# Issuing the product of queries and state straight behind the products of the inverse, in a gated-delta and attention trunk

## The chip, the cores and the metric

The kernel runs on one core of a Trainium2 chip, in one launch. The metric is the device time of an execution in microseconds. The time before is the median of three runs. The engines are named as in the profile: PE is TensorE (PEld its weight loads), DVE is VectorE, ACT is ScalarE, POOL is GpSimd, SP is the engine that issues the DMAs. Each engine takes its instructions in the order in which they stand in its queue, and holds at an instruction whose semaphore has not come yet.

## What is computed

One sequence of 1024 tokens with 1024 channels goes through two layers. The first is a gated DeltaNet layer (16 value heads of width 128, 8 key heads, each of which serves two value heads), the second a forgetting-attention layer; both have a gate path, an output projection and a conditioning by adaLN. The change concerns the scan of the first layer:

```python
def step(state, inp):
    q_n, k_n, u_n, w_n, a_n, gl_n = inp
    v_new = u_n - jnp.einsum('bhcd,bhde->bhce', w_n, state)
    o = (jnp.einsum('bhcd,bhde->bhce', q_n, state)
         + jnp.einsum('bhcs,bhse->bhce', a_n, v_new))
    state = state * gl_n[..., None, None] + jnp.einsum('bhcd,bhce->bhde', k_n, v_new)
    return state, o
```

Here `u` and `w` come out of the inverse of a unit triangular matrix, of which there is one for each head and chunk. All of it is float32.

## The kernel before

The tokens are taken in two halves of 512, and the value heads in pairs that share a key head (8 groups). So the first layer has 16 units of work, one for each half and group, and each unit has four chunks of 128 tokens. For a unit the kernel projects k, q, v and the gate (float32 split into two float32r parts, three products each, tile `mm`), convolves them, builds the triangular matrices, inverts them by blocks (partly by DVE and small DMAs, then by `invert_merge` on PE), and at last runs `chain`, which walks through the four chunks with the state of the group.

In `chain` a chunk uses one bank of PSUM called `ch`, of which there is only one buffer. Its left half (columns 0 to 255) first takes the product of keys and state (L1000). DVE reads that half and makes `xp` (L1004). Two products with the blocks of the inverse, `r`, fill the right half (L1011). ACT reads the right half and makes `vn` (L1018), DVE reads it and makes `ve` (L1022). Then the product of queries and state is written to the left half (L1027), and ACT scales it into `qe` (L1031). A second bank, `co`, takes the two products with `vn` (L1039) and the product of keys with `ve` (L1041), from which DVE makes the new state (L1048) and the output of the chunk, `og` (L1056). Accesses to one bank by different engines are kept one after another, also where they touch different columns of it; the semaphores for that follow from the order in which the accesses stand in the program.

PE's order is set by hand, by the planner `Flow`. Each piece of work is a generator that yields a planned distance in ns; `Flow` adds a planned cost for every product and resumes, by priority, whichever generator is due. The distances behind the steps of a chunk are `Y_C0` = 2700 (behind `xp`), `Y_C1` = 2200 (behind the product of queries and state), `Y_C3` = 1300 (behind the products with `vn`) and `Y_C2` = 1700 (behind the state). Between the steps the planner puts projection products and other units' work. PE thus goes through a fixed list. The orders of DVE, ACT, POOL and SP are not written by hand: a scheduler sets them from a simulated run of the whole program.

Of the kernel before, what the change touches and what calls it, by code (L numbers as in the profile page):

```python
# [28 lines left out]
def bc(ap, axis, n):  # L29
    a = ap.unsqueeze(axis)  # L30
    shape = list(a.shape)
    shape[axis] = n
    return a.broadcast_to(shape)
# [74 lines left out]
class Flow:  # L108
# [21 lines left out]
    def mm(self, out, lhsT, rhs, start=True, stop=True):  # L130
        self.t += self._cost(lhsT, rhs)
        self.nc.tensor.matmul(out, lhsT, rhs, start=start, stop=stop)  # L132
# [54 lines left out]
def tile_trunk(  # L187
# [27 lines left out]
    mm, tr_ = flow.mm, flow.tr  # L215
# [297 lines left out]
    with ExitStack() as sa:  # L513
# [3 lines left out]
        def at(shape, name, bufs=1, dt=F32):  # L517
            return pa.tile(shape, dt, name=name, tag=name, bufs=bufs)

        def pst(tag, bufs):  # L520
            return flow.bank(tag, bufs, lambda: psa.tile([P, 512], F32, name=tag, tag=tag, bufs=bufs))
# [351 lines left out]
        def chain_all():  # L873
            for i in range(2 * NG):
                yield from hold(lambda: done["merge"] > i and done["prep2"] > i and done["prep"] > i)
                yield from chain(ts[i])
# [110 lines left out]
        def chain(t):  # L987
            h, g, gt, kf, r = t["h"], t["g"], t["gt"], t["k"], t["r"]
            ktok, qf, am, uv, epo, ex = t["ktok"], t["q"], t["am"], t["uv"], t["epo"], gt["ex"]
            wn, wex, neg = t["wn"], t["wex"], gt["neg"]  # L990
            st = state[g]
            og = at([P, CPH, 2, P], "og", 2)
            so = at([P, CPH, 2], "so", 2)
            for c in range(CPH):
                first = h == 0 and c == 0
                p1 = yield from pst("ch", 1)
                if first:
                    xp = uv[:, c].rearrange("p j f -> p (j f)")
                else:
                    mm(p1[:, 0:256], kf[:, c], st)  # L1000
                    xt = at([P, 2 * P], "xp", 2)
                    for j in range(2):
                        sl = slice(j * P, (j + 1) * P)
                        nc.vector.scalar_tensor_tensor(  # L1004
                            xt[:, sl], p1[:, sl], neg[:, c, 2 * g + j : 2 * g + j + 1], uv[:, c, j],
                            op0=ALU.mult, op1=ALU.add,
                        )
                    xp = xt
                    yield Y_C0
                for j in range(2):  # L1010
                    mm(  # L1011
                        p1[:, 256 + j * P : 256 + (j + 1) * P], r[:, j * CPH + c],
                        xp[:, j * P : (j + 1) * P],
                    )
                vn = at([P, 2 * P], "vn", 2)
                ve = at([P, 2, P], "ve", 2)
                for j in range(2):
                    nc.scalar.activation(  # L1018
                        vn[:, j * P : (j + 1) * P], p1[:, 256 + j * P : 256 + (j + 1) * P], AF.Copy,
                        scale=wn[:, c, j : j + 1],  # L1020
                    )
                nc.vector.tensor_tensor(  # L1022
                    ve, p1[:, 256:512].rearrange("p (j f) -> p j f", f=P),
                    bc(wex[:, c], 2, P), op=ALU.mult,
                )
                if not first:
                    mm(p1[:, 0:256], qf[:, c], st)  # L1027
                    qe = at([P, 2 * P], "qe", 2)
                    for j in range(2):
                        sl = slice(j * P, (j + 1) * P)  # L1030
                        nc.scalar.activation(  # L1031
                            qe[:, sl], p1[:, sl], AF.Copy, scale=ex[:, 1, c, 2 * g + j : 2 * g + j + 1]
                        )
                flow.free(p1, R_C + 1000)
                yield Y_C1
                p2 = yield from pst("co", 1)
                for j in range(2):
                    sl = slice(j * P, (j + 1) * P)
                    mm(p2[:, sl], am[:, j, c], vn[:, sl])  # L1039
                yield Y_C3  # L1040
                mm(p2[:, 256:512], ktok[:, c], ve.rearrange("p j f -> p (j f)"))  # L1041
                for j in range(2):
                    sl = slice(j * P, (j + 1) * P)
                    s2 = p2[:, 256 + j * P : 256 + (j + 1) * P]
                    if first:
                        nc.vector.tensor_copy(st[:, sl], s2)
                    else:
                        nc.vector.scalar_tensor_tensor(  # L1048
                            st[:, sl], st[:, sl], ex[:, 2, c, 2 * g + j : 2 * g + j + 1], s2,
                            op0=ALU.mult, op1=ALU.add,  # L1050
                        )
                oc = og[:, c].rearrange("p j f -> p (j f)")
                if first:
                    nc.scalar.copy(oc, p2[:, 0:256])
                else:
                    nc.vector.tensor_tensor(oc, p2[:, 0:256], qe, op=ALU.add)  # L1056
                for j in range(2):
                    jk = at([P, P], "sqt", 1, BF16)
                    nc.scalar.activation(jk, og[:, c, j], AF.Square, accum_out=so[:, c, j : j + 1])
                flow.free(p2, R_C)  # L1060
                yield Y_C2
            done["core"] += 1
            t["out"] = og, so
# [833 lines left out]
```

## Time and profile before

| | |
|---|---|
| median of 3 runs | 2116.97 us (2114.73 to 2119.29) |
| profiled execution | 2123.97 us, of which the span is 2122.0 |
| PE busy | 1885.7 us, 89% of the span |
| PEld busy | 1571.7 us, 74% |
| DVE busy | 1343.5 us, 63% |
| ACT busy | 1035.7 us, 49% |
| mean granted clock of PE | 0.947 |
| products of `ch`, first to last start | 185.4 to 1221.2 us |

In the profile all products stand under line L132 and all transposes under L136, the lines of the planner's two helpers, so they are told apart by the tiles that they write and read: `ch<-state,q` is the product of queries and state, `ch<-state,k` that of keys and state, `ch<-xp,rmat` those with the inverse. A float32 product makes two records, a float32r product one. "Idle before" is the time for which an engine had nothing to do ahead of an instruction, and the name behind the arrow is what ended it.

### The profile page before, as it was taken

Reading aid. Unit: us, or ns where it says so; the run is one execution under the profiler, and the core shown is the slowest. Engines: PE = TensorE matmul, PEld = TensorE weight load, DVE = VectorE, ACT = ScalarE, POOL = GpSimd, SP = SyncE. Lnnn points to the kernel's source line nnn. Section 1 sums busy time; section 2 is a strip of 40 time slices with the busy share of each in tenths; the row PEclk is TensorE's granted clock in tenths of the full one; section 3 lists DMA queues with packets and bytes.
Section 4 is the critical chain, followed back from the end, with each engine's and each line's share of the span. In section 5 each row is a group of like instructions: output and inputs, shape, how many; then the busy total and the mean of one; then the engine's idle time right before and its main releaser. Section 6 shows DMA issues by size and latency. Waiting matters only on the chain. (4 is left out here: it accounts for less than half of the span.)

```text
span 2122.0 us, 35794 instructions
## 1 busy us (share of the span) xinstructions
PE 1885.7 (89%) x12892; PEld 1571.7 (74%) x12892; DVE 1343.5 (63%) x3321; ACT 1035.7 (49%) x2672; POOL 367.1 (17%) x402
## 2 busy tenths in 40 slices
PE   4999798887888888888888888999999999999898
PEld 4777677666766676667766666878898888889676
DVE  6676877676667556756564556746666566566764
ACT  4455566454544344535444335426556556555631
POOL 1110111000101000000000024332322322321222
PEclk6889999898999899999999999999999999999999
DMA  6576456656545445434437899601101101111522
GB/s 247 200 225 210 151 195 205 191 187 199 178 157 155 144 126 162 151 118 145 128 89 244 261 323 338 210 12 60 61 26 55 60 31 50 60 41 47 173 80 93
DMA packets 222872, 307.15 MB, mean 145 GB/s; under 512 B 100396, under 2 KB 136876, under 8 KB 222696
## 3 DMA queue, kind: packets, MB, share of 16 engines
q1 hardware_dynamic: 222696, 304.88, 44.0%
q8 instruction: 101, 1.65, 0.3%
q14 instruction: 75, 0.61, 0.1%
HBM read 223.15 MB, written 81.67 MB: 144 GB/s over the span
## 5 line engine op out<-in xcount | busy, mean ns | idle before, releaser
L132 PE MATMUL mm<-ht_h,whi 128*128 128x512 f32 x768 | 356.8, 465 | 0.2 <-ACT cv_y L784 0.2
L132 PE MATMUL mm<-ht_l,whi 128*128 128x512 f32 x768 | 316.3, 412 | 0.0
L132 PE MATMUL mm<-ht_h,wlo 128*128 128x512 f32 x768 | 316.3, 412 | 0.0
L132 PE MATMUL mm<-whi,h_h 128*128 128x384 f32 x512 | 186.9, 365 | 0.9 <-DVE kn L1486 0.9
L132 PEld LDWEIGHTS mm<-ht_h,wlo 128*128 128x128 f32 x768 | 153.8, 200 | 36.7
L132 PEld LDWEIGHTS mm<-ht_h,whi 128*128 128x128 f32 x768 | 155.0, 202 | 30.2 <-issue 1.7
L132 PEld LDWEIGHTS mm<-ht_l,whi 128*128 128x128 f32 x768 | 155.4, 202 | 26.1
L132 PE MATMUL mm<-whi,h_l 128*128 128x384 f32 x512 | 172.9, 338 | 0.0
L132 PE MATMUL mm<-wlo,h_h 128*128 128x384 f32 x512 | 172.7, 337 | 0.0
L1637 DVE TENSOR_TENSOR ptl<-pt,pth 128x512 fp32r<-128x512 f32 x192 | 106.3, 555 | 91.2 <-ACT pth L1636 89.2
L1636 ACT CAST pth<-pt 128x512 fp32r<-128x512 f32 x192 | 91.3, 477 | 138.2 <-PE pt L136 137.5
L792 DVE SCALAR_TENSOR_TENSOR cv_y<-cv_t,conv_h,cv_y 128x512 f32<-128x512 f32 x192 | 144.1, 750 | 22.0 <-ACT cv_y L784 19.7
L132 PE MATMUL ch<-state,q 128*128 128x256 f32 x112 | 44.9, 487 | 111.5 <-DVE ve L1022 111.5
L331 DVE TENSOR_TENSOR wlo<-ht_h,whi 128x512 fp32r<-128x512 f32 x124 | 95.0, 806 | 62.6 <-ACT whi L328 50.3
L1601 ACT ACTIVATE lg<-lg,mx 128x896 f32<-128x896 f32 (+7 forms) x128 | 99.5, 777 | 55.2 <-DVE mx L1593 49.5
L1480 POOL TENSOR_TENSOR rs<-ss,mhalf 128x4 f32<-128x4 f32 x64 | 64.5, 1008 | 330.7 <-DVE ss L1478 319.7
L328 ACT CAST whi<-ht_h 128x512 fp32r<-128x512 f32 x124 | 70.8, 618 | 96.9 <-PE mm L132 40.4
L132 PEld LDWEIGHTS ch<-state,q 128*128 128x128 f32 x112 | 18.6, 208 | 122.2 <-DVE ve L1022 122.2
L132 PE MATMUL mm<-h_h,whi 128*128 128x512 f32 x240 | 99.9, 416 | 0.7 <-DVE wlo L1736 0.3
L132 PEld LDWEIGHTS mm<-whi,h_h 128*128 128x128 f32 x512 | 97.9, 191 | 3.5 <-ACT v L1482 1.2
L132 PEld LDWEIGHTS mm<-wlo,h_h 128*128 128x128 f32 x512 | 97.3, 190 | 2.0
L136 PE MATMUL pt<-ident,lg 128*128 128x128 f32 (+1 forms) x584 | 95.6, 272 | 3.1 <-ACT lg L1601 3.1
(373 smaller groups left out, 4658.5 us busy)
## 6 DMA issues: line engine op xcount, KB each, us to landing
ht_h<-in_wa_o_dram SPq DMA_DIRECT2D x62, 512.0 KB, 5.7
wc<-whi SPq DMA_DIRECT2D x45, 512.0 KB, 4.5
wc<-wlo SPq DMA_DIRECT2D x45, 512.0 KB, 4.2
wlo<-wc SPq DMA_DIRECT2D x45, 512.0 KB, 5.3
whi<-wc SPq DMA_DIRECT2D x45, 512.0 KB, 3.7
wlo<-in_wa_c_dram SPq DMA_DIRECT2D x35, 512.0 KB, 5.2
nx<-in_ada_w_dram SPq DMA_DIRECT2D x64, 256.0 KB, 3.0
wraw<-in_wb_dram SPq DMA_DIRECT2D x56, 256.0 KB, 2.7
```

The costliest lines, as they stand in the source:

```text
L132: self.nc.tensor.matmul(out, lhsT, rhs, start=start, stop=stop)
L136: self.nc.tensor.transpose(out, src, ident)
L328: nc.scalar.copy(hi, src)
L331: (lo_eng or nc.gpsimd).tensor_tensor(lo, src, hi.bitcast(F32), op=ALU.subtract)
L792: nc.vector.scalar_tensor_tensor(y, raw[:, j : j + HALF], w[:, j : j + 1], y, op0=ALU.mult, op1=ALU.add)
L1480: nc.gpsimd.tensor_tensor(rs, ss, mhalf[:, 0:4], op=ALU.pow)
L1601: nc.scalar.activation(lg, lg, AF.Exp, scale=-1.0, bias=mx[:, hh : hh + 1], accum_out=sums[:, tt : tt + 1],)
L1636: nc.scalar.copy(ph_[:, cs], pp[:, cs])
L1637: nc.vector.tensor_tensor(pl_[:, cs], pp[:, cs], ph_[:, cs].bitcast(F32), op=ALU.subtract)
```

## The change

The statement that issues the product of queries and state moves up by one step: it stands right behind the two products with the inverse, ahead of `vn` and `ve`. It stays left out in the first chunk of the first half, where there is no state. All planned distances and costs, and all tiles and buffers, are as they were.

```diff
                         p1[:, 256 + j * P : 256 + (j + 1) * P], r[:, j * CPH + c],
                         xp[:, j * P : (j + 1) * P],
                     )
+                if not first:
+                    mm(p1[:, 0:256], qf[:, c], st)
                 vn = at([P, 2 * P], "vn", 2)
                 ve = at([P, 2, P], "ve", 2)
                 for j in range(2):
...
                     bc(wex[:, c], 2, P), op=ALU.mult,
                 )
                 if not first:
-                    mm(p1[:, 0:256], qf[:, c], st)
                     qe = at([P, 2 * P], "qe", 2)
```

From L1029 on, the lines of the changed kernel have numbers higher by one; L1018 has become L1020, and L1022 has become L1024.

On PE nothing moves. In the 26th chunk that has this product, PE's rows before are these, each with the semaphores that it waits for in brackets (the semaphore of DVE is `DVE_49`, that of ACT `Activation_49`):

```order
L132 MATMUL ch<-xp,rmat_130 128x128 [waits DVE_49]
L132 MATMUL ch<-xp,rmat_130 128x128
L132 MATMUL ch<-state_141,q 128x256 [waits DVE_49]
L132 MATMUL mm<-ht_h,whi 128x512
...
L132 MATMUL su<-k 128x128 [waits PE_49]
...
L132 MATMUL co<-vn,d_6369 128x128 x2
```

And now:

```order
L132 MATMUL ch<-xp,rmat_130 128x128 [waits DVE_49]
L132 MATMUL ch<-xp,rmat_130 128x128
L132 MATMUL ch<-state_141,q 128x256
L132 MATMUL mm<-ht_h,whi 128x512
...
L132 MATMUL su<-k 128x128 [waits Activation_49]
...
L132 MATMUL co<-vn,d_6369 128x128 [waits Activation_49] x2
```

The order is the same; the product of queries and state has lost its wait for DVE, and later products, which needed no wait of their own behind it, have their own wait now.

On DVE, the same chunk, before (`nh` is a part of the adaLN products, fed by DMA, and `cv_y` the convolution):

```order
L1004 SCALAR_TENSOR_TENSOR xp_7766<-ch_7764,g_neg_2734,vtok_6845 128x128
L792 SCALAR_TENSOR_TENSOR cv_y_7754<-cv_t_7753,conv_h_110,cv_y_7754 128x512 [waits Activation_49,Pool_49]
...
L792 SCALAR_TENSOR_TENSOR cv_y_7754<-cv_t_7753,conv_h_110,cv_y_7754 128x512 [waits DVE_49]
L277 SCALAR_TENSOR_TENSOR nh_7681<-nx_8089,cond_84,nh_7681 128x512 [waits DMAHW2_49]
L792 SCALAR_TENSOR_TENSOR cv_y_7754<-cv_t_7753,conv_h_110,cv_y_7754 128x512 [waits DVE_49]
...
L1022 TENSOR_TENSOR ve_7820<-ch_7764,wex_6585 128x256 [waits Activation_49]
L277 SCALAR_TENSOR_TENSOR nh_7681<-nx_8133,cond_84,nh_7681 128x512 [waits DMAHW4_49,DVE_49]
```

And now:

```order
L1004 SCALAR_TENSOR_TENSOR xp_7766<-ch_7764,g_neg_2734,vtok_6845 128x128
L277 SCALAR_TENSOR_TENSOR nh_7681<-nx_7979,cond_84,nh_7681 128x512 [waits DMAHW7_49,DVE_49]
L792 SCALAR_TENSOR_TENSOR cv_y_7754<-cv_t_7753,conv_h_110,cv_y_7754 128x512 [waits Activation_49,Pool_49]
...
L792 SCALAR_TENSOR_TENSOR cv_y_7754<-cv_t_7753,conv_h_110,cv_y_7754 128x512 [waits DVE_49] x2
...
L1024 TENSOR_TENSOR ve_7821<-ch_7764,wex_6585 128x256 [waits PE_49,Activation_49]
L277 SCALAR_TENSOR_TENSOR nh_7681<-nx_8033,cond_84,nh_7681 128x512 [waits DMAHW2_49]
```

The scheduler has set an earlier `nh` in this place, so the adaLN products stand later against the chain than before; `ve` keeps its place behind the convolution. On ACT the rows of this chunk keep their order (`vn`, the tanh of L796, `qe`), and `qe` now waits for DVE instead of PE:

```order
L1020 ACTIVATE vn_7820<-ch_7764,wn_6584 128x128 [waits DVE_49,PE_49]
L1020 ACTIVATE vn_7820<-ch_7764,wn_6584 128x128
L796 ACTIVATE cv_t_7753<-cv_y_7754 128x512 [waits DVE_49,Pool_49]
L1032 ACTIVATE qe_7825<-ch_7764,g_ex_2730 128x128 [waits DVE_49]
```

The bank is now handed on in this order: the products with the inverse, the product of queries and state, `vn`, `ve`, `qe`. Over the whole program some hundred places on ACT and on SP, and more on DVE, have changed their order in this way by a few instructions.

## The prediction

> **What bounds the kernel now.** The product of queries and state is issued only while the gated-delta chains run, between 185 and 1222 us of the span, so I read that stage first, as one window:
>
> ```profile
> core 0: us, PE busy (x) PEld busy (x) DVE busy (x) ACT busy (x) POOL busy (x), PEclk, DMA share, GB/s
> 185.00:1222.00 1037.00, 882.53 (x7299) 710.87 (x7288) 664.43 (x1723) 490.18 (x1464) 88.78 (x135) 0.93 0.53 168
> ```
>
> TensorE (PE) is busy for 882.5 of 1037 us, so it idles 154.5. VectorE (DVE) is busy 664.4 / 1037 = 64% of the stage, ScalarE (ACT) 47%, the DMA engines 53%: PE is the engine nearest to its bound. What its idle time waits for stands in the list of waits, PE alone, same window (us in total, times, longest):
>
> ```profile
> PE ch L132 <- DVE ve L1022: 111.5, 56, 4.3
> PE ch L132 <- DVE state L1048: 16.5, 8, 3.8
> PE ch L132 <- DVE xp L1004: 5.8, 8, 1.6
> PE ch L132 <- DVE state L1046: 5.5, 3, 3.2
> PE su L132 <- DVE tmat L1201: 4.2, 2, 2.4
> PE co L132 <- ACT vn L1018: 1.0, 1, 1.0
> PE mm L132 <- ACT cv_y L784: 0.2, 1, 0.2
> ```
>
> One wait makes 111.5 of the 154.5 us: 56 times, in every chunk that has this product, 2.0 us on average. The last row matters too: the projections, the bulk of PE's work, wait for nothing, so there is always work behind the waiting product, and PE is in order. How the wait comes about is seen in the timeline of a quiet chunk (start, length, what, idle before):
>
> ```profile
> 711.06 0.59 PE L132 MATMUL ch<-state,k 128*128 128x256 f32 x2
> 711.31 0.59 PE L132 MATMUL mm<-ht_h,whi 128*128 128x512 f32 x1
> 711.73 0.40 PE L132 MATMUL mm<-ht_l,whi 128*128 128x512 f32 x1
> ...
> 714.95 0.60 PE L132 MATMUL ch<-xp,rmat 128*128 128x128 f32 x4
> 715.59 0.63 ACT L1018 ACTIVATE vn<-ch,wn 128x128 f32<-128x128 f32 x2 [2.01 <-PE ch L132]
> 716.25 0.42 DVE L1022 TENSOR_TENSOR ve<-ch,wex 128x256 f32<-128x256 f32 x1 [0.24 <-ACT vn L1018]
> 716.73 0.70 PE L132 MATMUL ch<-state,q 128*128 128x256 f32 x2 [1.18 <-DVE ve L1022]
> 717.47 0.63 ACT L1031 ACTIVATE qe<-ch,g_ex 128x128 f32<-128x128 f32 x2 [0.71 <-PE ch L132]
> ```
>
> The accesses to the bank go one after another: inverse products, vn on ACT, ve on DVE, then q times state on PE. 1.18 us is the least it can be: 0.63 for vn, 0.42 for ve and three handovers. Where ACT and DVE have other work queued ahead, it grows, as in a chunk further on:
>
> ```profile
> 730.27 0.71 PE L132 MATMUL ch<-xp,rmat 128*128 128x128 f32 x4 [0.61 <-DVE xp L1004]
> 731.82 0.63 ACT L1018 ACTIVATE vn<-ch,wn 128x128 f32<-128x128 f32 x2
> 733.42 0.41 DVE L1022 TENSOR_TENSOR ve<-ch,wex 128x256 f32<-128x256 f32 x1
> 733.89 1.22 PE L132 MATMUL ch<-state,q 128*128 128x256 f32 x2 [2.90 <-DVE ve L1022]
> 735.34 0.63 PE L132 MATMUL mm<-ht_l,whi 128*128 128x512 f32 x1
> 735.76 0.63 PE L132 MATMUL mm<-ht_h,wlo 128*128 128x512 f32 x1
> 737.47 1.76 PE L132 MATMUL su<-k 128*128 128x128 f32 x8
> 739.30 0.39 PE L132 MATMUL mm<-ht_l,whi 128*128 128x512 f32 x1
> 739.53 0.39 PE L132 MATMUL mm<-ht_h,wlo 128*128 128x512 f32 x1
> 739.76 0.60 PE L132 MATMUL co<-vn,d 128*128 128x128 f32 x4
> 742.27 0.59 PE L132 MATMUL co<-ve,ktok 128*128 128x256 f32 x2
> ```
>
> The wait has a second price here. After it the 512-wide products start 0.42 us apart (735.34 to 735.76), later 0.23 (739.30 to 739.53): PE runs at half its clock for a while. I looked for all half-clock stretches in the stage whose preceding 3.4 us contained this wait, and asked for the windows of those 22 (first, one between, last, sum):
>
> ```profile
> 254.26:257.67 3.41, 3.41 (x18) 3.32 (x16) 2.96 (x12) 1.15 (x3) 0.00 (x0) 0.50 0.64 237
> ...
> 732.12:738.95 6.83, 5.06 (x15) 4.31 (x16) 3.81 (x10) 1.58 (x5) 0.41 (x1) 0.50 0.39 127
> ...
> 1203.16:1206.57 3.41, 3.33 (x8) 2.68 (x9) 0.02 (x1) 0.63 (x2) 0.00 (x0) 0.50 0.88 262
> sum 109.20, PE 98.48 PEld 78.93 DVE 51.63 ACT 33.85 POOL 6.29; mean PE 4.48 PEld 3.59 DVE 2.35 ACT 1.54 POOL 0.29
> ```
>
> So 109.2 us pass at a granted clock of 0.50, with PE busy for 98.5 of them.
>
> **The change, part by part.** No instruction is added or dropped, and PE's order stays the same row for row; what goes is the product's wait. Term 1 is the row itself: **-111.5 us**.
>
> Term 2 is the clock. A product takes 0.42 us instead of 0.23 in the half-clock stretches, so of 98.5 busy us 1 - 0.23 / 0.42 = 45% are lost: 44.6 us. Some stretches may stay, since tiny merge products and other waits also leave PE idle; I take **-38 us**, between 0 and -45.
>
> The Trainium skill, "TensorE: Matmul & The Clock Gate", section "Why this matters for your kernels", says that PE loses its clock after one idle window, and advises against idle gaps over about 3 us. By that rule few of these waits (2.0 us on average) would cost any clock, and term 2 would be near 0. The trace disagrees: a wait of 2.90 us was followed by a window at 0.50, so I go by the trace.
>
> Term 3 is what the readers pay. vn now waits for q times state as well. Its price when nothing holds it up is that of the like-shaped k product: 711.06 to 711.73 less one 512-wide product of 0.23 = 0.44 us. vn, ve and qe shift by that much after the inverse products, and queued behind them on ACT are tanh and copies of the projections (0.59 to 0.69 us each), whose bank is not short by the last row of the waits. Who waits for vn and ve on PE are the two products into the next bank. In the busy chunk at 730 PE would go on at about 731.4 and do 9 products of 0.23 and the eight su<-k (1.5 us at half clock, so about 0.8) before it needs vn: about 734.3. vn ended at 732.45 and would end at 732.9 at the latest: 1.4 us to spare. ve ended at 733.83 and would at 734.3; PE needs it 2.5 us after vn, at 736.8. These distances cover the new waits; without them each chunk would pay up to the old 2.0 us again. The one row that has this wait now shows 1.0 us. I take **+2 us**, with 0 and 56 x 1.18 = 66 as ends.
>
> Term 4 is what else comes due, since PE no longer pauses while DVE and ACT catch up. The stage would shrink to about 925 us with the same DVE work, 664 / 925 = 72% busy instead of 64%; DVE's free share falls from 36% to 28%, and its delays grow. PE waits for DVE's xp and state already, 16.5 + 5.8 + 5.5 = 27.8 us in 19 waits. I let these grow to about 50, **+22 us**, and the small waits inside the inverse's merges by **+4**. The ends are 0 (the order adapts) and 80 (three times what stands there now, on top).
>
> Waits cost clock too: at 38 / 111.5 = 0.34 us per us, the 28 us of new ones cost **+10**.
>
> The moved order on DVE and SP has one place that could hurt, the inverse's blocks that come back by DMA. Of the 16 units the one with the shortest distance has these rows:
>
> ```profile
> 569.26 1.78 DVE L1147 STREAM_TRANSPOSE tmat<-rmat 32x256 f32<-32x256 f32 x4 [2.50 <-DMA rmat<-rb]
> ...
> 582.57 0.20 PE L132 MATMUL su<-tmat,d 16*32 16x16 f32 x2
> ```
>
> The blocks are in place at 571.04, PE takes them 11.5 us later. Over the 3.5 chunks of a unit PE gains about 3.5 x (2.0 + 0.7) = 9 us, and the distance is renewed with every unit: I take 0.
>
> **Sum.** -111.5 - 38 + 2 + 26 + 10 = -111.5 us. The profiled execution took 2123.97 us, 2122.0 of it span, so 2012.5; it stood 7.0 above the median of 2116.97, so the forecast for the median is **2005 us**.
>
> **Rivals.** (a) *Nothing comes back*: the chain has slack at every step, and terms 3 and 4 are 0. For it speak the 1.4 and 2.5 us to spare; against it the xp row, where PE already waits in 8 chunks. 2117 - 111.5 - 44.6 = 1961 us.
>
> (b) *The clock stays*: half-clock windows come as often without this wait. For it speak the mean clock of 0.93, which other waits share; against it that 22 stretches follow this wait. 2117 - 111.5 + 28 = 2033 us. This is also what the skill's rule on idle windows would give.
>
> (c) *The wait moves on*: DVE cannot keep up, and xp, state and vn take over 60% of the stall, 67 us, with only 15 us of clock won. 2117 - 111.5 + 67 - 15 = 2057 us. For it speaks that DVE works through waits of its own, against it its 28% of free time.
>
> (d) *Slower*: the am-times-vn product (L1039) becomes the new stall, and a longer one, because vn now starts behind q times state, behind whatever the scheduler has put ahead on ACT. It decides once PE loses more there than the (111.5 + 38) / 56 = 2.7 us that a chunk gains; at 3.5 us the sum is 2117 + 56 x 0.8 = 2162. The 1.4 us to spare in a busy chunk speak against it: vn would have to slip by over 4 us each time.
>
> (e) *No change*: the wait is put back under another name ahead of the same work, about 2117 us. Only the bank's first reader could carry it, and that is not on PE.
>
> **How the numbers follow.** Chances: forecast 56%, (a) 17%, (b) 9%, (c) 12%, (d) 4%, (e) 2%. The range from **1960 to 2055** holds the forecast, (a), (b) and the better part of (c). Faster by over 0.2% (about what the spread of the runs allows to tell from no change) are the forecast, (a), (b) and (c): 94%; same 2%, slower 4%.
>
> **What would show it.** Right: the wait of PE for ve is gone or has become a wait of a few us of the state-update product; PE's idle time between 185 us and the end of the chains falls from 154 to about 70 us; the mean clock there rises from 0.93 to 0.96 or more; vn starts about 0.44 us later behind the inverse products; the stages behind it keep their lengths. Wrong in term 3 if co<-vn waits for ACT more than some us in all; wrong in term 4 if the waits for xp and state stay near 28 or pass 80; wrong in term 2 if the clock stays at 0.93 with PE's idle time gone.

## The result

The changed kernel takes 1984.77 us (median of 3 runs, 1981.06 to 1987.19) where the kernel before took 2116.97. The ratio is 0.937, with a 95% interval from 0.9345 to 0.9402: 6.3% or 132 us faster. The forecast was 2005 us, with a range from 1960 to 2055. The profiled execution took 1981.06 us, of which 1979.3 are span, so the two profiled executions differ by 142.9 us.

First the engines' busy time over the whole execution, to be read beside PE's 1885.7 us of before, and then two windows: the stage, from 185 us to the end of the last product of queries and state, and from there to the end:

```profile
PE 1838.8 (93%) x12892; PEld 1536.0 (78%) x12892; DVE 1334.9 (67%) x3321; ACT 1030.6 (52%) x2672; POOL 375.2 (19%) x402
```

```profile
core 0: us, PE busy (x) PEld busy (x) DVE busy (x) ACT busy (x) POOL busy (x), PEclk, DMA share, GB/s
185.00:1079.70 894.70, 833.18 (x7234) 676.14 (x7233) 654.28 (x1721) 483.12 (x1456) 96.78 (x134) 0.97 0.61 194
1079.70:1979.30 899.60, 857.07 (x4700) 733.82 (x4699) 557.10 (x1312) 456.88 (x989) 251.43 (x208) 0.99 0.30 101
```

The stage ends 142 us earlier (at 1079.7 instead of 1221.6 us), and what follows it has its old length, 899.6 us instead of 900.4. In the stage the clock rises from 0.93 to 0.97, and PE's idle time falls from 154.5 us to 894.7 - 833.2 = 61.5. Over the whole span PE idles 1979.3 - 1838.8 = 140.5 us instead of 2122.0 - 1885.7 = 236.3, 95.8 less, and it is busy for 46.9 us less, with the same 12892 records. These two make the 142.7 us by which the span is shorter. Here are PE's waits in the stage now (total, times, longest):

```profile
PE ch L132 <- DVE state L1049: 19.0, 10, 4.1
PE ch L132 <- DVE state L1047: 7.8, 3, 3.6
PE su L132 <- DVE tmat L1148: 4.8, 4, 2.6
PE mm L132 <- DMA olo<-ogl_d: 4.1, 3, 1.8
PE ch L132 <- DVE xp L1004: 3.7, 3, 2.7
PE tr L136 <- DVE vt L799: 3.5, 1, 3.5
PE tr L136 <- DVE k L799: 3.0, 1, 3.0
PE mm L132 <- DMA ohi<-og_d: 2.9, 3, 1.9
```

The row of 111.5 us is gone, and no row of its size has come in its place. The same busy chunk that the prediction worked through, the 26th, now reads so in the timeline:

```profile
662.49 0.71 PE L132 MATMUL ch<-xp,rmat 128*128 128x128 f32 x4
663.04 0.60 PE L132 MATMUL ch<-state,q 128*128 128x256 f32 x2
663.28 0.58 PE L132 MATMUL mm<-ht_h,whi 128*128 128x512 f32 x1
664.42 0.62 ACT L1020 ACTIVATE vn<-ch,wn 128x128 f32<-128x128 f32 x2
664.86 1.05 PE L132 MATMUL su<-k 128*128 128x128 f32 x8
665.36 0.42 DVE L1024 TENSOR_TENSOR ve<-ch,wex 128x256 f32<-128x256 f32 x1
665.82 0.62 ACT L1032 ACTIVATE qe<-ch,g_ex 128x128 f32<-128x128 f32 x2
666.45 0.61 PE L132 MATMUL co<-vn,d 128*128 128x128 f32 x4
668.99 0.59 PE L132 MATMUL co<-ve,ktok 128*128 128x256 f32 x2
```

PE does not pause, vn is ready at 665.04 and is needed at 666.45, and ve is ready at 665.78 and needed at 668.99.

The quiet chunk of the prediction, the 25th, has these rows now (the third, of ACT, is from the same stretch):

```profile
651.75 0.60 PE L132 MATMUL ch<-xp,rmat 128*128 128x128 f32 x4
652.72 0.20 PE L132 MATMUL su<-tmat,d 16*32 16x16 f32 x2
652.83 0.62 ACT L1020 ACTIVATE vn<-ch,wn 128x128 f32<-128x128 f32 x2 [2.45 <-PE ch L132]
```

vn starts 652.83 - 651.75 = 1.08 us behind the first product with the inverse, where it was 715.59 - 714.95 = 0.64: 0.44 us later, as forecast.

### The profile page after: what moved, and what is told of

Same layout as the page of the kernel before. It is cut to its first block, busy times and chain, and to the rows that moved or that the text cites. A ratio compares the mean times of both kernels' runs of the same rounds, so it can differ in the third digit from the quotient of the medians.

```text
span 1979.3 us, 35876 instructions
## 1 busy us (share of the span) xinstructions
PE 1838.8 (93%) x12892; PEld 1536.0 (78%) x12892; DVE 1334.9 (67%) x3321; ACT 1030.6 (52%) x2672; POOL 375.2 (19%) x402
## 4 chain that ended last, share of the span: by engine, by line
PE 60%; DVE 15%; DMA 14%; ACT 4%; issue 3%; SPq 3%; POOL 2%; DVEq 0%; POOLq 0%; ACTq 0%
PE mm L132 38%; PE lg L132 5%; PE oT L132 3%; PE pt L136 3%; DMA nx<-in_ada_w_dram 3%; PE su L132 3%; PE tr L136 3%; PE ch L132 2%; DVE wlo L331 2%; DMA lb<-d 1%; PE co L132 1%; DMA lr<-lb 1%; DMA ohi<-og_d 1%; DVE cv_y L792 1%; DVE d L929 1%
## 5 line engine op out<-in xcount | busy, mean ns | idle before, releaser
L132 PE MATMUL mm<-ht_h,whi 128*128 128x512 f32 x768 | 346.2, 451 | 0.2 <-ACT cv_y L784 0.2
L132 PE MATMUL mm<-ht_l,whi 128*128 128x512 f32 x768 | 308.3, 401 | 0.9 <-POOL ht_l L331 0.8
L132 PE MATMUL mm<-ht_h,wlo 128*128 128x512 f32 x768 | 308.6, 402 | 0.0
L132 PEld LDWEIGHTS mm<-ht_h,wlo 128*128 128x128 f32 x768 | 148.8, 194 | 34.5
L132 PEld LDWEIGHTS mm<-ht_h,whi 128*128 128x128 f32 x768 | 149.9, 195 | 28.6 <-issue 1.7
L132 PEld LDWEIGHTS mm<-ht_l,whi 128*128 128x128 f32 x768 | 149.9, 195 | 26.6 <-POOL ht_l L331 2.0
L132 PEld LDWEIGHTS mm<-whi,h_l 128*128 128x128 f32 x512 | 96.1, 188 | 0.0
L132 PE MATMUL mm<-h_h,wlo 128*128 128x512 f32 x240 | 94.3, 393 | 0.0
```

## The experiments

Ratios are to the kernel before, run on the same chip in the same series, with 95% intervals. The changed kernel stood at 0.937 in its first series.

**The wait taken away by distance instead.** The product stays where it was in the program, and the planner puts other work ahead of it:

```diff
                 if not first:
+                    yield Y_C1 - 200
                     mm(p1[:, 0:256], qf[:, c], st)
...
-                yield Y_C1
+                yield Y_C1 if first else 200
                 p2 = yield from pst("co", 1)
```

> The product of queries and state stays behind vn and ve in the program, as before, but the planner puts 2000 ns of other work on PE ahead of it (and 200 instead of 2200 behind it, so a chunk's planned length is the same). Theory (PE's pause alone is the price, where the bank's accesses stand does not matter): the wait for ve falls from 111.5 us to some 20 to 30, since only the longer of the 56 waits outlast the distance, and most of the half-clock time goes with it: 1995 to 2020 us. Rival 1 (the gain comes from the order in which the bank is handed on, or from what the scheduler made of DVE, ACT and SP in the changed kernel): no such gain, 2090 us or more. Rival 2 (vn being later costs the changed kernel something): this one is faster than the changed kernel's 1985 us.

Measured: ratio 0.954 (0.950 to 0.957), which is 2019 us on the scale of 2116.97, at the upper end of what was expected; the median was 2025.83 in a series whose kernel before stood at 2125.74. PE's largest waits in the stage:

```profile
PE ch L132 <- DVE ve L1022: 24.1, 20, 3.3
PE ch L132 <- DVE state L1049: 20.9, 14, 4.7
PE mm L132 <- DMA ohi<-og_d: 6.1, 4, 3.0
```

Three quarters of the gain come without any change in the order of the bank's accesses, so what counts is that PE need not stand still. Rival 1 falls in its main part, the order of the bank. That the orders which the scheduler set anew on DVE, ACT and SP add or take a little is not tested by itself. Rival 2 falls as it was put, since this kernel is not the faster one. The wait that is left, 24.1 us in 20 chunks, is that of the chunks whose wait outlasts 2 us of distance, as expected. With the clock that such waits cost (0.954 here, 0.966 with the change) it is most of the difference between the two. Moving the statement removes the wait whatever its length; a distance removes it up to that distance.

**The move in the second half alone.** The first half's products keep their place:

```diff
-                if not first:
+                if h == 1:
                     mm(p1[:, 0:256], qf[:, c], st)
                 vn = at([P, 2 * P], "vn", 2)
...
                 if not first:
+                    if h == 0:
+                        mm(p1[:, 0:256], qf[:, c], st)
                     qe = at([P, 2 * P], "qe", 2)
```

> The move is made in the second half's units alone: 32 of the 56 products lose their wait, 24 keep it. Theory: the waits add up chunk by chunk, and so does the gain. The 32 hold about 63 of the 111.5 us, so the kernel gains about 0.57 x 132 = 75 us, 2042 us, and the wait for ve that is left is about 48 us in 24. Rival (the gain hangs on the scan running without any pause, or comes back as the waits shift): under 50 us or over 100 us of gain.

Measured: ratio 0.962 (0.957 to 0.968), a gain of 79 us on 2117. The wait left is that of the 24 products that kept it:

```profile
PE ch L132 <- DVE ve L1024: 48.9, 24, 3.7
```

The gain adds up by chunks: 32 of 56 products give 60% of the 132 us. It needs no scan that runs without a pause, and little of it comes back elsewhere: the row fell by 62.6 us, and PE idles for 58 us less over the span (178.2 instead of 236.3).

**The pause filled with idle work.** The kernel before, with five products that nothing needs in the time of the wait (they write the bank `co`, which is overwritten later):

```diff
+                p2 = yield from pst("co", 1)
+                if not first:
+                    for _ in range(5):
+                        nc.tensor.matmul(p2, identb, bc(identb, 1, 4), start=True, stop=True)
                 vn = at([P, 2 * P], "vn", 2)
...
-                p2 = yield from pst("co", 1)
```

> The kernel before, with five idle bf16 products of 512 columns (about 0.22 us each, 1.1 us in all) between the products of the inverse and the product of queries and state, into the bank co, which the chunk overwrites later. They add work that no output needs, inside the time in which PE would wait anyway (1.17 us at least). Theory (the pause costs twice, once as idle time and once as half clock behind it): the end of each wait stays where it was, the wait row falls by about 56 x 1.1 = 60 us as PE is busy instead, half-clock time falls to less than half of its 140 us, and the kernel gets faster though it does more: 2070 to 2095 us. Rival (the half clock behind a wait costs nothing, as DVE sets the pace there): within 10 us of 2117.

Measured: ratio 0.979 (0.975 to 0.983), 44 us faster, with more to do. Its rows are, in order, the engines' busy time on the page, span and clock, and the groups of the two products within the stage (busy, mean ns, idle before):

```profile
PE 1912.0 (92%) x13172; PEld 1569.3 (75%) x13172; DVE 1336.7 (64%) x3321; ACT 1034.1 (50%) x2672; POOL 374.3 (18%) x402
```

```profile
core 0: 2081.8 us, clock 0.965
```

```profile
L1018 PE MATMUL co<-identb 128*128 128x512 bf16 x280 | 71.0, 385 | 0.0
L132 PE MATMUL ch<-state,q 128*128 128x256 f32 x112 | 40.3, 443 | 56.6 <-DVE ve L1026 55.0
```

The 71.0 us of the idle products lie in part over the records next to them. Without them, PE's records cover 1850.6 us of this execution, where they covered 1885.7 before, and PE's other products stand in the same order. So the kernel's own work took 35 us less. Of these, 4.6 are the product's own records (44.9 us before, 40.3 here), and the other 30 go with the clock: its mean rose from 0.947 to 0.965, and the stage has 58 us at half clock instead of 140, less than half, as expected. The wait fell by 56 us, whose place the idle products took. So the wait's second price shows by itself, in a kernel that does more work: some 30 us for the half of the wait that was filled, where the prediction had worked out 44.6 for the whole. The rival, on which this time is hidden behind DVE, falls.

**Twice the product.** The changed kernel issues the product of queries and state two times:

```diff
                 if not first:
+                    nc.tensor.matmul(p1[:, 0:256], qf[:, c], st, start=True, stop=True)
                     mm(p1[:, 0:256], qf[:, c], st)
```

> The changed kernel with the product of queries and state issued twice (the second writes the same result over the first). PE has 56 x 0.44 = 25 us more to do, and vn, ve and qe start another 0.44 us later. Theory (vn has time to spare, PE sets the pace): the kernel gets slower by those 25 us and no more, ratio to before about 0.949, and co<-vn waits for ACT under 5 us in all. Rival (the readers of the bank are near their limit): the products with vn and ve wait, 40 us or more slower, 0.956 or above.

> The changed kernel once more, beside the other three on the same chip: 0.937 of the kernel before, within 0.003.

Measured, in one series: the changed kernel again, 0.9335 (0.931 to 0.936), a little below its first series, with intervals that overlap; with the product twice, 0.937 (0.934 to 0.941), 8 us more, with intervals that overlap a little. So the readers of the bank are not near their limit. But the theory's 25 us are not there either:

```profile
PE 1857.5 (93%) x13004; PEld 1555.8 (78%) x13004; DVE 1333.4 (67%) x3321; ACT 1031.7 (52%) x2672; POOL 373.0 (19%) x402
```

```profile
core 0: 1989.5 us, clock 0.969
```

Beside the changed kernel of this series (PE busy 1840.4 us of 1976.6, clock 0.965) PE is busy for 17 us more and idle for 1989.5 - 1857.5 = 132.0 instead of 136.2. Added work on PE is paid in part by waits that it replaces (4 us here) and by a higher clock (0.969 instead of 0.965). "PE sets the pace" was too simple: what ends the stage is PE's work together with the waits that its static order makes for it.

**More work on DVE.** In the changed kernel the last step of each convolution is done twice:

```diff
-            nc.vector.scalar_tensor_tensor(dst, tv, 1.0, yv, op0=ALU.add, op1=ALU.mult)
+            for _ in range(2):
+                nc.vector.scalar_tensor_tensor(dst, tv, 1.0, yv, op0=ALU.add, op1=ALU.mult)
```

> The changed kernel with the last step of each convolution (L799, 0.69 us on DVE) done twice, 64 times: 44 us more work on DVE in the first layer, none of it on the state's chain, though k, q and v come 0.69 us later. Theory of the forecast's term 4 (what comes back is set by DVE's free share, which this takes down from 27% to about 22%): PE's waits for xp and state grow by 10 us or more, the kernel gets slower by 10 to 30 us, ratio 0.942 to 0.951. Rival (DVE is far enough from its limit; what came back has other causes): within 6 us of the changed kernel, 0.934 to 0.940.

Measured: ratio 0.946 (0.942 to 0.950) beside 0.9335 for the changed kernel, 26 us slower. The added rows sum to 44 us, for which DVE is busy for 34.7 us more (1370.5 instead of 1335.8). So DVE does set a part of PE's time in this stage; whether by its load, or because k, q and v come later, this run does not tell apart. The profiled execution is the slowest of the four, 2013.79 us where the median is 2003.98, so its waits may be larger than usual. PE's waits, and the same rows of the changed kernel in this series below:

```profile
PE ch L132 <- DVE state L1050: 21.6, 12, 3.8
PE su L132 <- DVE tmat L1149: 11.4, 4, 7.2
PE ch L132 <- DVE state L1048: 10.9, 4, 4.0
PE tr L136 <- DVE vt L800: 7.6, 4, 5.6
PE ch L132 <- DVE xp L1005: 4.9, 4, 2.5
```

```profile
PE ch L132 <- DVE state L1049: 17.1, 9, 3.4
PE ch L132 <- DVE state L1047: 8.0, 3, 3.6
PE su L132 <- DVE tmat L1148: 5.9, 4, 4.1
PE ch L132 <- DVE xp L1004: 3.9, 3, 2.7
PE tr L136 <- DVE vt L799: 3.3, 1, 3.3
```

The waits for xp and state grow by 8.4 us (29.0 to 37.4), a little under the 10 that the theory asked for, and those for vt and for the inverse's blocks (tmat) by 9.8; the clock falls to 0.955. The work on DVE counts, but it shows at the inverse and at v as much as in the chain.

**Four other distances on top of the change.** Each tries to take away a wait that the changed kernel has left.

```diff
-Y_C2 = 1700
+Y_C2 = 2700
```

> The changed kernel with Y_C2 = 2700 instead of 1700: 1 us more work on PE between a chunk's state product and the next chunk's product of keys and state. Theory (what is left of PE's idle time in the scan is mostly the wait for the state, 27 us in 13, and PE has other work to put there): that wait falls to under 10 us, and the kernel gains 10 to 25 us, 1960 to 1975 us. Rival (a longer chunk takes the scan past the projections that fill it): slower than 1985 us.

```diff
-Y_C1 = 2200
+Y_C1 = 1700
...
-Y_C2 = 1700
+Y_C2 = 2200
```

> The changed kernel with Y_C1 = 1700 instead of 2200 and Y_C2 = 2200 instead of 1700: half a us of PE's other work is moved from ahead of vn's products to ahead of the next product of keys and state, with the same length of a chunk. Theory (the wait for the state, 27 us, is what is left, and vn has over 1 us to spare): that wait falls to about 18 us, co<-vn waits stay under 4 us, 5 to 10 us faster than the changed kernel, 0.932 to 0.935. Rival (as with the longer Y_C2 alone, waits turn up elsewhere for it): no gain, 0.937 or above.

```diff
+                mm(p2[:, 256:512], ktok[:, c], ve.rearrange("p j f -> p (j f)"))
                 for j in range(2):
                     sl = slice(j * P, (j + 1) * P)
                     mm(p2[:, sl], am[:, j, c], vn[:, sl])
-                yield Y_C3
-                mm(p2[:, 256:512], ktok[:, c], ve.rearrange("p j f -> p (j f)"))
...
-                yield Y_C2
+                yield Y_C2 + Y_C3
```

(In this third one the statement of ve stands ahead of that of vn, too.)

> The changed kernel with ve ahead of vn, and the product of keys and ve ahead of those of vn, which follow at once; the distance Y_C3 that stood between them goes behind the state. A chunk's length on PE is the same, the state has 1300 ns more until it is needed. Theory (the state waits, 26 us, are the largest part of PE's idle time left in the scan, and come off without a cost when the distance is only moved): they fall under 8 us, 10 to 20 us faster than the changed kernel, ratio 0.925 to 0.932. Rival (as when distances were changed before, PE's waits turn up at other places, since DVE's queue is what is late): ratio 0.934 or above.

```diff
-LAT = 40000
+LAT = 46000
```

> The changed kernel with the planned distance from a unit's matrix to the use of its inverse longer by 6 us (LAT 46000 instead of 40000). Theory (without the pauses PE comes to some of the merges before the blocks are there: about 10 us of waits of the products su and tr for tmat): these waits fall under 4 us and 5 to 10 us are won, ratio 0.930 to 0.933. Rival: no gain, 0.934 or above, as the wait is replaced.

Measured: 0.943 (0.939 to 0.947), 0.939 (0.935 to 0.943), 0.937 (0.933 to 0.941) and 0.940 (0.937 to 0.944). The changed kernel itself had 0.937 in its first series and 0.9335 beside the second of these; the first, third and fourth ran in series without it. None is faster than the changed kernel, and the third is as fast as its first series. Each took away the wait at which it aimed, wholly or in part; in the third one, for instance, the state waits of 26.8 us are nearly gone (the last row here), and these stand in their place:

```profile
PE su L132 <- DVE tmat L1147: 8.4, 2, 8.2
PE ch L132 <- DVE xp L1004: 7.6, 4, 2.9
PE su L132 <- DVE tmat L1176: 7.6, 5, 4.3
PE mm L132 <- DMA ohi<-og_d: 6.5, 6, 2.1
PE co L132 <- ACT vn L1024: 6.1, 6, 1.6
PE co L132 <- DVE ve L1019: 6.0, 7, 1.3
...
PE ch L132 <- DVE state L1048: 1.8, 2, 1.0
```

All four rivals stood: what is won at one wait is lost at others. A part of the loss lies behind the stage, where the list of its waits does not show it. Here are the third one's windows:

```profile
185.00:1057.70 872.70, 814.32 (x7179) 662.11 (x7178) 646.37 (x1712) 474.62 (x1446) 93.95 (x134) 0.97 0.61 192
1057.70:1987.80 930.10, 873.09 (x4749) 747.48 (x4747) 561.41 (x1321) 462.55 (x997) 248.81 (x209) 0.98 0.31 104
```

Its stage ends 22 us earlier than that of the changed kernel (1079.7), but what follows takes 930.1 us instead of 899.6. PE is busy there for 16 us more, with 49 more records (the stage has 55 fewer), and idles for 14 us more. In the first two, too, what follows the stage takes 18 to 21 us more, and in the fourth 9. Which of DVE's queue, the DMAs and the planner's fill sets the place of each new wait, these runs don't tell apart. The best version found is the changed kernel as it stands.

## Why the prediction was right

The mechanism was as forecast, and the time fell by more. The sum of 111.5 us for the profiled execution came out as 142.9. The 31 us between them are three misses on the same side: the clock (8), the product's shorter records, for which there was no term (10.5), and what else comes due, with vn's wait (12). Term by term:

**Term 1, the wait**: -111.5 us forecast, and that row is gone. The run on the second half alone shows that it adds up by chunks, and the run with the distance that it goes, for the most part, with the pause and not with the order of the bank.

**Term 2, the clock, with its counterpart for new waits**: -38 and +10, so -28 net. PE is busy for 46.9 us less. 10.5 us of these are the product's own records, as the groups of the whole span show (before, then after):

```profile
L132 PE MATMUL ch<-state,q 128*128 128x256 f32 x112 | 44.9, 487 | 111.5 <-DVE ve L1022 111.5
```

```profile
L132 PE MATMUL ch<-state,q 128*128 128x256 f32 x112 | 34.4, 390 | 0.0
```

The other 36 us go for the most part with the clock: the mean of the span went from 0.947 to 0.966. Another way to count bears it out: in the half-clock stretches of the whole span PE was busy for 188.7 us before and for 105.8 now, and 45% of the difference is 37 us. Forecast was 28, so the term was too small by 8: I had let a part of the windows stay for a reason of caution, and had counted 28 us of new waits against it, of which 15.7 came. The idle products show that the clock is not lost in proportion to the wait. There, half of the wait is still in place (55.0 us), and the mean clock is 0.965, nearly that of the changed kernel; what counts is how the idle time is spread, as the last section shows. So rival (b), on which the clock stays as it is, falls. With it falls the rule on gaps of over about 3 us, as the prediction had it from the Trainium skill, "TensorE: Matmul & The Clock Gate", section "Why this matters for your kernels": of the 22 half-clock stretches, 12 stand behind a wait of less than 3 us. The stretch that the prediction showed from 732.12 us on begins within the wait of 2.90 us, 1.1 us after its start, and not behind it. Another passage fits: the Trainium skill, "TensorE: Matmul & The Clock Gate", section "A second HAM failure mode: psum-queue depth-cycling". By it short idle times between groups of products, when they are frequent, make the clock swing. This trace agrees, with 109.2 us at half clock behind 22 waits of 2.8 us on average (all 56 average 2.0).

**A term that was missing**: PE restarts after the wait, and the products on both sides of it no longer run into each other. In the quiet chunk before, 717.36 - 714.95 = 2.41 us passed from the first product with the inverse to the row behind the product of queries and state (that row, the first of the merge, is below). Of these 1.18 were idle, so 1.23 us of work. In the same chunk now (its rows are in the section on the result) the same work takes 652.72 - 651.75 = 0.97, so 0.26 less. In the 41 chunks that run at full clock in both executions it is 0.27 us less in the median, and 11.2 us together. So of the 46.9 us, some 11 to 15 are restarts and 32 to 36 the clock. This is worked out from rows; no run measured the restart apart from the clock.

```profile
717.36 0.20 PE L132 MATMUL su<-tmat,d 16*32 16x16 f32 x2
```

**Term 3, vn later**: +2 us. The two products into `co` wait 0.9 us in all (the groups of the changed kernel's stage, below), and the busy chunk has 1.4 us to spare for vn, as worked out, and 3.2 for ve, where 2.5 had been worked out. With the product doubled, which shifts the readers once more, the wait for vn is 1.3 us, where the changed kernel of that series has 1.0. Rival (d), the slower one, had its point of decision 2.7 us per chunk away.

```profile
L132 PE MATMUL co<-vn,d 128*128 128x128 f32 x252 | 39.3, 278 | 0.8 <-ACT vn L1020 0.8
L132 PE MATMUL co<-ve,ktok 128*128 128x256 f32 x126 | 38.9, 390 | 0.1
```

**Term 4, what else comes due**: +26 us. All of PE's other idle time grew by 111.5 - 95.8 = 15.7 us. This is the term that was mis-sized most, and its place was wrong too. It had let the waits for xp and state grow from 27.8 to 50. They went to 30.5: state from 22.0 to 26.8, and xp fell from 5.8 to 3.7. The prediction itself had named this as the sign that term 4 is wrong (these waits stay near 28). The small waits of the merges grew by some 3 us, about as forecast. The rest turned up where the prediction had nothing: the parts of the outputs that come back by DMA for the output projection (olo and ohi, 7.0 us in the stage, 0.2 before), v and k. That DVE's share of busy time would bring the new waits in the chain was the step that failed: the share rose to 654.3 / 894.7 = 73%, close to the 72% worked out, but the chain's waits hardly moved. More work on DVE can cost PE time (26 us in the run that added it); that DVE's load is what brought back the 15.7 us is not shown. So rival (c) falls by its size: 15.7 us came back, not 67. Rival (a), 1961 us, falls too, since something did come back; the measured 1985 us lies about midway between it and the forecast of 2005, because of the restarts, the clock and the smaller term 4. Rival (e), no change, falls with the time.

## What to carry to other kernels

Where several engines share a bank and their accesses are kept in program order, and an in-order engine's next write to it goes to columns that the others do not read, put that write ahead of their reads if its operands are there. Its queue then does not wait for them, and the reads moved by the length of the write alone here (0.44 us). Price a wait of PE at more than its length, by looking at the granted clock in the windows behind it; here 36 us of clock went with 95.8 us of idle time, 0.4 for each idle us on average. Once a stall of this kind was gone here, cutting a smaller wait in the static order moved it, in four tries of four, in part to behind the stage. A shorter row in the list of waits is no gain until the time shows it.

## What the hardware showed

22 half-clock stretches with 109.2 us stood behind this one wait, which was between 1.2 and 4.3 us long there; 34 of the 56 waits, up to 2.8 us long, had none behind them. What mostly tells the two apart in this trace is the idle time of a whole stretch. In the stage the clock changes at times that lie a multiple of 3.41 us apart. Cut at these times, the stage before has 305 stretches. Of those in which PE idled for 1.8 us or more, 25 of 26 were followed by one at half clock; of those with 1.2 to 1.8 us, 9 of 28; of those with less, 7 of 251. The changed kernel's stage has 10 stretches with 1.8 us or more, 9 of them followed by half clock, and the kernel with idle products 15, with 13. So a little work put into each wait can save most of the clock, though half of the wait stays.

That kernel, with 280 useless products in these waits, was 44 us faster than without them. And 25 us of work added to PE in the changed kernel cost 8 us, with intervals that overlap a little: PE was busy for 17 us more, idle for 4 less, and its clock was 0.969 instead of 0.965.
